# A hybrid decoder step on one core: the first stage's instructions in a fixed order, planned from estimated times, and the cached rows copied in other stages

## The chip, the cores and the metric

The kernel runs on 1 core of one Trainium2 chip. The metric is the device time of one execution in microseconds (us). The engines are PE (TensorE, with its weight loads as PEld), DVE (VectorE), ACT (ScalarE), POOL (GpSimd) and SP, whose queue issues all DMA transfers here. Each engine works through its own instructions in their order; semaphores make it wait for others.

## The reference, cut to what matters

Two layers over 512 prompt tokens and 8 sample tokens, each with its own cached state. Layer 0 mixes by gated DeltaNet, layer 1 by dilated sliding-window attention; each is followed by an MLP with a squared ReLU.

```python
for i in range(DEPTH):                      # DEPTH = 2
    hp, hs = rmsnorm(yp, norm_mix[i]), rmsnorm(ys, norm_mix[i])
    if i % N_MIXERS == 0:
        op, cbp, sp = gdn_mixer(hp, conv0, s0, *wts)
        osm, cbs, ss = gdn_mixer(hs, state_conv[j], state_gdn[j], *wts)
    else:
        op, bufs_p = dsw_prompt(hp, *wts)
        osm, bufs_s = dsw_sample(hs, (cache_kv_w128[j], cache_kv_w512[j], cache_kv_w2048[j]), *wts)
    yp, ys = yp + op, ys + osm
    yp = yp + sqrelu_mlp(rmsnorm(yp, norm_mlp[i]), mlp_w_up[i], mlp_w_down[i])
    ys = ys + sqrelu_mlp(rmsnorm(ys, norm_mlp[i]), mlp_w_up[i], mlp_w_down[i])
```

In `gdn_mixer`, projections give q, k, v, a gate z and two figures per head; q, k and v go through a convolution of width 4 and SiLU. There are 8 q/k heads and 16 value heads. In chunks, the state of each value head follows from an inverse of a unit triangular matrix:

```python
t_inv = triangular_solve(eye + a_strict, eye, lower=True, unit_diagonal=True)
u = t_inv @ (v * beta); w = t_inv @ (kb * exp(gc)); attn = (q @ k.T) * decay
def step(s, inp):                           # one chunk after the other
    v_new = u_c - w_c @ s
    o = qg_c @ s + a_c @ v_new
    s = s * gl_c + kd_c.T @ v_new
```

The sample's k/v buffers are results too: the cached rows, moved up by one where the window is full, and the new row behind them.

## The kernel before, in words

All of it is fp32. A dense projection is made of three matmuls of rounded halves: the weights are split into `whi` (rounded, by ACT) and `wlo` (the rest, by DVE), the tokens likewise, and `proj` (L157) adds high by high, high by low and low by high. A tile of 128 output features and 8 blocks of input is 2 halves of 260 tokens, 24 matmuls each, 48 together. A raw weight tile has 512 KB; three are held (`WB`), and two of each half.

The stages follow each other: `load_x`, `gdn` (layer 0's mixer, the "first stage"), `mlp`, `dsw` (layer 1's mixer, "attention"), `mlp`, `store_x`.

The first stage goes by pairs p = 0 to 7: one q/k head and its two value heads. For each pair:

- `key` (K), `query` (Q) and `values` (V, two tiles) project and convolve by `project` (L505); `gates` (Z, two tiles) makes silu(z).
- `decay` (L588) loads rows of cumulated log-decay from DRAM (`ET<-Dg`), subtracts on DVE (L596), and makes E from the products `kk` of keys with keys.
- `invert` (L622) sends E's diagonal blocks through DRAM (`D<-E`, then `Ft<-D`), solves them on POOL in 62 steps (L638, L641: `fs` and `held`), and sends the result back (`D<-held`, `held<-D`) into the tile `Uf`. `merge` (L649) makes blocks of 64 and 128 on PE (`px`, `pu`).
- `scan` (L698) is the recurrence: per chunk of 128 tokens `pk` on PE, `R` on DVE, `pv` on PE, `vn` on ACT, `pS` and `po` on PE, `S` on DVE.
- `sample` (L796) is the step of the 8 sample tokens: products `sks` with the cached states `S`, then `u` sent through DRAM to all partitions (`sut`, `ut`, `Du`, `ub`) and the states updated on ACT and POOL.
- `out` (L847) is norm, gate and split; `out_proj` (L878) adds the output projection of a pair to the residual stream.

Before pair 0 the stage makes its constants: the small projection `bafm`, its transpose `bat`, beta and the log-decay (with a polynomial on POOL, L451 and L452), the cumulated sums `gc`, their transposes to DRAM (`gcT`, `Dg`) and the sample's figures `sbc`.

What order the instructions take is decided by a scheduler that builds each engine's list from a simulated time line, with raised priority for `decay`, `invert`, `merge`, `scan`, `sample` and `out` (`urgent`, L33). Beside each weight load, `weights` (L134) issues one copy of cached rows from DRAM to DRAM (`kept_rows`, L88; 136 copies of up to 832 KB) once `owed` has gone from -16 to 1. So 52 copies fall in the first stage, 64 in the first MLP and 20 in attention.

In attention, head h's projections stand beside head h-1's scores and values (rounds 0 to 8); the output projections of pairs of heads are made in round 8 (`DOUT`), the last behind it.

Of the kernel before, what the change touches and what calls it, by code (L numbers as in the profile page):

```python
# [10 lines left out]
F32 = mybir.dt.float32  # L11
# [18 lines left out]
HP = {"decay": 2000, "invert": 2000, "merge": 2000, "scan": 2000, "sample": 2000, "out": 2000}  # L30


def urgent(f):  # L33
    def g(self, *a):
        with self.tc.high_priority(HP[f.__name__]):
            return f(self, *a)

    return g

KEEP = 104  # L40
WARM = 24
RAW = 6
SMALL = 1300
WB = (3, 2, 2)
MM = 2
OHB = 8
DOUT = {8: ((0,), (1, 2))}
PACE = dict(gdn=1, mlp0=1, dsw=1, mlp1=1)


class Common:
    """What every stage uses: constants, the residual stream, the weight stream, projections."""

    def __init__(self, ctx, tc, I, O):
# [7 lines left out]
        # what lives as long as the kernel: the residual stream and constants, and the split operand  # L62
# [9 lines left out]
        self.kept, self.owed, self.stage = self.kept_rows(), -16, "gdn"  # L72
        self.gain = {}
# [14 lines left out]
    def kept_rows(self):  # L88
        """The cached rows that stay in the sample's k/v buffers, a piece of them at each step."""
# [18 lines left out]
    def bank(self, name, tag="misc", n=512):  # L108
        return self.ps.tile([P, n], F32, tag=tag, name=name, bufs=self.tags[tag])
# [24 lines left out]
    def weights(self, cols, nk=KT):  # L134
        """cols: DRAM [nk * 128, n] pieces; gives each 128 columns in parts for the products."""
# [3 lines left out]
        for c in cols:  # L139
            for j in range(0, c.shape[1], step):  # L140
# [6 lines left out]
                self.owed += PACE[self.stage]  # L147
                while self.owed >= 1:
                    self.owed -= 1
                    next(self.kept, None)  # L150
# [5 lines left out]

    def proj(self, w, mov, evac, m=P, halves=(0, 1)):  # L157
        nc = self.nc
        nk = len(mov)
        for hf in halves:  # L160
            ps = self.pm.tile([P, H], F32, tag="mm", name="mm", bufs=MM)
            s = slice(hf * H, hf * H + H)
            for k in range(nk):
# [4 lines left out]
            evac(ps[:m], hf, s)  # L168
# [4 lines left out]
    def split_x(self, gain, k, hf, x=None):  # L173
        """The moving operand of the next projection, x * gain, as a rule not normalized yet."""
        nc = self.nc
        x = self.x if x is None else x
        s = slice(hf * H, hf * H + H)
        nc.scalar.activation(self.xh[:, k, s], x[:, k, s], AF.Copy, scale=gain[:, k : k + 1])  # L178
        nc.vector.scalar_tensor_tensor(  # L179
            self.xl[:, k, s], x[:, k, s], gain[:, k : k + 1], self.xh[:, k, s].bitcast(F32), ALU.mult, ALU.subtract  # L180
# [15 lines left out]
    def mean_sq(self, acc):  # L196
        """1 / (mean square + eps) by token: [128, 5], the last column for the sample tokens."""
# [13 lines left out]
    def rsqrt(self, pool, x, eng, tag):  # L211
        """1 / sqrt(x) for positive x [128, n], by Newton's iteration from an estimate made of its bits."""
# [12 lines left out]
    def bcast(self, pool, r, tag="bc"):  # L225
        """A figure by token, [128, 5], over all partitions: [128, T]."""
# [21 lines left out]
    # the tensor engine's clock goes up with use: let it run while the rows come in  # L248
# [107 lines left out]
def gdn(K, l, rms, gain, done):  # L356
# [9 lines left out]
    with ExitStack() as ctx:  # L366
# [4 lines left out]
        for k in range(KT):  # L371
            nc.gpsimd.tensor_tensor(xn[:, k], K.x[:, k], rb, ALU.mult)
# [1023 lines left out]
```

## Time and profile before

| | |
|---|---|
| median of 3 runs | 2167.4 us (2167.13 to 2167.78) |
| span of the profiled execution, its own time | 2168.5 us, 1.1 us over that median |
| PE busy | 1989.6 us (92%) |
| DVE busy | 1349.5 us (62%) |
| ACT busy | 899.4 us (41%) |
| POOL busy | 535.6 us (25%) |
| moved by DMA | 328.54 MB |

All comes from one profiled execution. "Busy" counts time in which an instruction of the engine runs; matmuls overlap each other, so PE's work is better read from the distance of their starts. A line number is that of the kernel, and many lines are those of a helper; names such as `mm<-split,whi` are result and operands. "Waits" name the event that came last before an instruction could start.

### The profile page before, as it was taken

How to read it: one execution, taken by the hardware profiler on the slowest of the kernel's cores; microseconds unless marked ns; L12 is line 12 of the kernel's file. 1: busy time of each engine (PE TensorE's matmuls, PEld its weight loads, DVE VectorE, ACT ScalarE, POOL GpSimd, SP SyncE). 2: the span in 40 equal slices, each digit the busy share in tenths (PEclk: the TensorE clock that was granted, in tenths of full speed). 3: DMA queues.
4: the chain of work that ended last, by engine and by line, in shares of the span. 5: the costliest groups of instructions: out<-in, count | busy, mean ns of one | idle time of the engine just before them, and what ended most of it. 6: DMA issues, size and time to landing. Idle time of an engine off the chain costs nothing. (4 is left out here: it accounts for less than half of the span.)

```text
span 2168.5 us, 41683 instructions
## 1 busy us (share of the span) xinstructions
PE 1989.6 (92%) x16361; PEld 1950.9 (90%) x16361; DVE 1349.5 (62%) x3332; ACT 899.4 (41%) x2416; POOL 535.6 (25%) x821
## 2 busy tenths in 40 slices
PE   7677889896969789999999999999999989999999
PEld 6677778896969679999999999999999989999998
DVE  6754856785766584544556467676766785544544
ACT  5434444444334353223244555555555444233231
POOL 4253264355253230000002133232332250000000
PEclk8889989988979889999999999999999999999999
DMA  5334554764655538666676675534445343333332
GB/s 145 68 71 114 149 157 127 223 181 128 204 150 158 168 96 303 228 238 242 232 248 227 221 242 141 140 108 123 120 128 137 97 115 88 89 98 89 94 92 79
DMA packets 416277, 328.54 MB, mean 152 GB/s; under 512 B 48408, under 2 KB 404568, under 8 KB 413896
## 3 DMA queue, kind: packets, MB, share of 16 engines
q1 hardware_dynamic: 416080, 325.88, 50.4%
q8 instruction: 128, 2.10, 0.4%
q14 instruction: 69, 0.57, 0.1%
HBM read 302.19 MB, written 132.83 MB: 201 GB/s over the span
## 5 line engine op out<-in xcount | busy, mean ns | idle before, releaser
L165 PE MATMUL mm<-split,whi 128*128 128x260 f32 (+1 forms) x2960 | 866.7, 293 | 3.8 <-ACT split L178 2.5
L167 PE MATMUL mm<-split,wlo 128*128 128x260 f32 (+1 forms) x2960 | 851.8, 288 | 9.4 <-DVE wlo L132 9.4
L166 PE MATMUL mm<-split,whi 128*128 128x260 f32 (+1 forms) x2960 | 851.8, 288 | 8.7 <-DVE split L179 8.6
L166 PEld LDWEIGHTS mm<-split,whi 128*128 128x128 f32 (+1 forms) x2960 | 567.1, 192 | 12.3 <-DVE split L179 10.5
L167 PEld LDWEIGHTS mm<-split,wlo 128*128 128x128 f32 (+1 forms) x2960 | 566.5, 191 | 11.8 <-DVE wlo L132 10.9
L165 PEld LDWEIGHTS mm<-split,whi 128*128 128x128 f32 (+1 forms) x2960 | 567.6, 192 | 7.2 <-ACT split L178 3.7
L132 DVE TENSOR_TENSOR wlo<-raw,whi 128x1024 fp32r<-128x1024 f32 (+1 forms) x273 | 341.0, 1249 | 195.3 <-ACT whi L131 177.7
L131 ACT CAST whi<-raw 128x1024 fp32r<-128x1024 f32 (+1 forms) x273 | 285.8, 1047 | 411.7 <-PE mm L166 396.1
L167 PE MATMUL mm<-hh,wlo 128*128 128x260 f32 x1024 | 288.8, 282 | 0.0
L166 PE MATMUL mm<-hl,whi 128*128 128x260 f32 x1024 | 288.8, 282 | 0.0
L165 PE MATMUL mm<-hh,whi 128*128 128x260 f32 x1024 | 288.1, 283 | 0.0
L167 PEld LDWEIGHTS mm<-hh,wlo 128*128 128x128 f32 x1024 | 193.0, 188 | 0.0
L166 PEld LDWEIGHTS mm<-hl,whi 128*128 128x128 f32 x1024 | 192.8, 188 | 0.0
L165 PEld LDWEIGHTS mm<-hh,whi 128*128 128x128 f32 x1024 | 192.3, 188 | 0.0
L335 DVE TENSOR_TENSOR t<-mm,bc 128x260 f32<-128x260 f32 x128 | 54.8, 428 | 153.0 <-PE mm L167 153.0
L191 POOL TENSOR_TENSOR acc<-acc,sq 128x260 f32<-128x260 f32 x42 | 37.8, 909 | 382.0 <-ACT sq L190 381.3
L638 POOL TENSOR_TENSOR fs<-Ft,held 128x60 f32<-128x60 f32 (+24 forms) x248 | 100.5, 405 | 89.2 <-DMA Ft<-D 58.7
L131 ACT CAST hh<-q 128x260 fp32r<-128x260 f32 x128 | 52.5, 410 | 122.1 <-DVE q L322 122.1
L165 PE MATMUL mm<-onh,whi 128*128 128x260 f32 x256 | 90.3, 356 | 13.0 <-DVE base L892 7.9
L530 DVE SCALAR_TENSOR_TENSOR conv<-pre,held,conv 128x512 f32<-128x512 f32 x96 | 77.6, 808 | 30.1 <-POOL pre L508 27.2
L641 POOL TENSOR_TENSOR held<-held,fs 128x60 f32<-128x60 f32 (+24 forms) x248 | 90.5, 365 | 18.5
L132 DVE TENSOR_TENSOR hl<-q,hh 128x260 fp32r<-128x260 f32 x128 | 54.9, 429 | 57.0 <-ACT hh L131 57.0
(374 smaller groups left out, 3319.4 us busy)
## 6 DMA issues: line engine op xcount, KB each, us to landing
out_dram<-in_cache_kv_w_dram SPq DMA_DIRECT2D x112, 832.0 KB
raw<-in_dsw_w_in_dram SPq DMA_DIRECT2D x72, 512.0 KB
raw<-in_mlp_w_up_dram SPq DMA_DIRECT2D x64, 512.0 KB
raw<-in_mlp_w_down_dram SPq DMA_DIRECT2D x64, 512.0 KB
raw<-in_gdn_w_in_dram SPq DMA_DIRECT2D x48, 512.0 KB
S<-in_state_gdn_dram SPq DMA_DIRECT2D x16, 512.0 KB
raw<-in_gdn_w_out_dram SPq DMA_DIRECT2D x16, 512.0 KB
ub<-Du SPq DMA_DIRECT2D x16, 512.0 KB
```

What stands on the lines that cost most here:

```text
L131: nc.scalar.copy(hi, src)
L132: nc.vector.tensor_tensor(lo, src, hi.bitcast(F32), ALU.subtract)
L165: nc.tensor.matmul(ps[:m], lhsT=w[0][:, k, :m], rhs=xh[:, s], start=k == 0, stop=False)
L166: nc.tensor.matmul(ps[:m], lhsT=w[0][:, k, :m], rhs=xl[:, s], start=False, stop=False)
L167: nc.tensor.matmul(ps[:m], lhsT=w[1][:, k, :m], rhs=xh[:, s], start=False, stop=k == nk - 1)
L191: nc.gpsimd.tensor_tensor(acc[:, s], acc[:, s], t, ALU.add)
L335: nc.vector.tensor_tensor(t, ps, r2[:, s], ALU.mult)
L530: nc.vector.scalar_tensor_tensor(a, pre[:, j : j + NP], convw[:, ft, j : j + 1], a, ALU.mult, ALU.add)
L638: nc.gpsimd.tensor_tensor(tmp[:, :m, :n], Ft[:, None, j + 1 :, j].to_broadcast([P, m, n]), Uo[:, :m, j : j + 1].to_broadcast([P, m, n]), A ...
L641: nc.gpsimd.tensor_tensor(Uo[:, :m, j + 1 :], Uo[:, :m, j + 1 :], tmp[:, :m, :n], ALU.add)
```

## The change

In the first stage the scheduler has no say any more. A class `Weave` wraps the engines: each call adds an estimated time to that engine's clock (per-engine constants: a DVE instruction 0.16 us and 0.00106 per element, a POOL one 0.24 and 0.002, a DMA issue 0.1), and instructions stand in the order in which they are called. The dense work is a stream written by hand (`ORDER`). After each k-block of three matmuls the planner looks at the chains (generators that stop at each `yield`) and lets those go on whose inputs are due by its clocks. Loads of raw tiles are issued three ahead, by `fetch`, as the planner reaches them. `LOAD`, `TO_INV` and `FROM_INV` are its figures for a load (6 us), the way of E to POOL (12) and back (9).

Within the stage: the output projections of pairs 0 and 1, 2 and 3, 4 and 5 are made together; key rows are kept as they are (`kt`) and the scan scales `vd` on ACT in place of two `kd` products on DVE; `pS` is one product of 256 columns; small POOL copies (`tail`) and memsets are gone; three PSUM banks rather than two take the projections; osb shares E's tile. Elsewhere: `PACE` sets the copies per weight load (first stage 0, first MLP 1, attention 0.5, second MLP 0.6: 64, 40 and 32 copies), and attention makes the output projection of the first pair of heads in round 6 rather than 8.

Names in the rows: `bat`, `gc`, `gcT`, `sbc` are the constants, `mm` a dense projection, `E`, `D`, `Ft`, `held` the inversion's tiles (`held` also other constants), `S` the sample's states, `raw` a weight tile.

First place: PE, at the constants of the first stage. Before, around `gc`:

```order
L167 MATMUL mm<-split,wlo 128x260
L165 MATMUL mm<-split,whi 128x260
L166 MATMUL mm<-split,whi 128x260
L167 MATMUL mm<-split,wlo 128x260
L463 MATMUL gc<-base,held 128x64
L464 MATMUL gc<-base 128x64
L165 MATMUL mm<-split,whi 128x260
```

Now:

```order
L534 MATMUL bat<-base,bafm 128x32 x4
L534 MATMUL bat<-base,bafm 8x32
L572 MATMUL gc<-base,held 128x64
L573 MATMUL gc<-base 128x64
L579 MATMUL gcT<-base,held 64x128
L598 MATMUL sbc<-sbd,base 128x256
L145 MATMUL mm<-split,wlo 128x260
L145 MATMUL mm<-split,whi 128x260 x2
```

Before, 123 rows of mostly dense products stand between `bat` and `gc`; now none, and the dense stream of K0 (but for its first two products) stands behind `sbc`.

Second place: DVE, at the first subtraction on `ET`. Before:

```order
L783 COPY base<-sst 128x16
L785 COPY base<-sst 128x8
L132 TENSOR_TENSOR wlo<-raw,whi 128x1024
L222 SCALAR_TENSOR_TENSOR base<-base 128x4
L596 TENSOR_TENSOR ET<-ET,held 128x1024
L534 SCALAR_TENSOR_TENSOR conv<-tanh,conv 128x512
```

Now:

```order
L583 TENSOR_TENSOR held<-held 128x64
L599 COPY held<-sbc 128x256
L145 TENSOR_TENSOR ET<-ET,held 128x1024
L145 TENSOR_TENSOR wlo<-raw,whi 128x1024 x2
L145 TENSOR_TENSOR held<-held,bc 128x512
```

Before, K0 is split, projected and convolved when `ET` comes; now the subtraction stands ahead of the split of K0's weights.

Third place: SP, around the inversion's result of a pair. Before (pair 0):

```order
L629 DMA D_576<-E 32x8x32 x4
L632 DMA Ft<-D_576 128x1x1024
L146 DMA raw<-in_gdn_w_in_dram 128x8x128 x3
L642 DMA D_577<-held 4x256x32
L146 DMA raw<-in_gdn_w_in_dram 128x8x128
L646 DMA held<-D_577 32x8x32 x4
```

Now (pairs 0 and 1):

```order
L145 DMA D_1254<-E 32x8x32 x4
L145 DMA Ft<-D_1254 128x1x1024
L145 DMA D_835<-held 4x256x32
L145 DMA held<-D_835 32x8x32 x4
L145 DMA Du<-ut 16x128
L145 DMA raw<-in_gdn_w_in_dram 128x8x128
L145 DMA ub<-Du 128x1024
L145 DMA raw<-in_gdn_w_in_dram 128x8x128 x2
L145 DMA out_dram<-S_1143 128x8x128
```

Raw tiles stand behind stores that wait for POOL (`D_835<-held`, `out_dram<-S_1143`) and behind loads that wait for such stores; the copies of cached rows, which stood among them, are gone from the stage.

The diff's core:

```diff
-HP = {"decay": 2000, "invert": 2000, "merge": 2000, "scan": 2000, "sample": 2000, "out": 2000}
+HOP, LOAD, TO_INV, FROM_INV, BACKLOG = 0.15, 6.0, 12.0, 9.0, 4.0
-MM = 2
-OHB = 8
-DOUT = {8: ((0,), (1, 2))}
-PACE = dict(gdn=1, mlp0=1, dsw=1, mlp1=1)
+MM = dict(gdn=3, mlp0=2, dsw=2, mlp1=2)
+OHB = 6
+DOUT = {6: ((0,),), 8: ((1, 2),)}
+PACE = dict(gdn=0, mlp0=1, dsw=0.5, mlp1=0.6)
+class Weave:
+    def spend(self, eng, us):
+        t = max(self.clk[eng], self.cur + (HOP if self.last not in (eng, None) else 0.0)) + us
+        self.clk[eng], self.cur, self.last = t, t, eng
+    def due(self, c):
+        if not self.done.issuperset(c[4].get("names", ())):
+            return None
+        tag = c[4].get("tag")
+        busy = 0.0 if c[1] < 0 else max(self.clk["vector"], self.clk["scalar"]) - BACKLOG
+        return max(c[0], self.free[tag][self.turn[tag]] if tag else 0.0, busy)
+    def dense(self, steps):
+        self.cur, self.last = self.now, "tensor"
+        for _ in steps:
+            self.pump()
+            self.cur, self.last = self.now, "tensor"
+    def need(self, *names):
+        while not self.done.issuperset(names):
+            t, _, i = min((max(t, self.now), c[1], i) for i, c in enumerate(self.chains) for t in (self.due(c),) if t is not None)
+            self.clk["tensor"] = t
+            self.step(self.chains[i])
+class Timed:
...
+                us = {"vector": 0.16 + 0.00106 * n, "scalar": 0.17 + 0.00087 * n, "gpsimd": 0.24 + 0.002 * n, "sync": 0.1}[self.name]
-        self.kept, self.owed, self.stage = self.kept_rows(), -16, "gdn"
+        self.kept, self.owed, self.stage = self.kept_rows(), 0, "gdn"
-OUTP = {p: [((p - 2,), 0, 8)] for p in range(2, 8)}
-OUTP[8] = [((6,), 0, 8), ((7,), 0, 8)]
-EARLY = (7,)
+ORDER = "K0 Q0 K1 Q1 V0 K2 Q2 Z0 V1 Z1 K3 Q3 V2 K4 Q4 Z2 O01 V3 K5 Q5 Z3 V4 K6 Q6 Z4 O23 V5 K7 Q7 Z5 V6 V7 Z6 O45 Z7 O6 O7"
+        def fetch():
+            if len(raws) < len(tiles):
+                c, nk = tiles[len(raws)]
...
+                nc.sync.dma_start(t, c.rearrange("(k p) n -> p k n", p=P))
+                raws.append((t, W.cur + LOAD))
+                K.keep()
-                kd = self.kd = K.tile(gp, [P, C4, 2, P], F32, tag="kd", name="kd", bufs=2)
-                for v in range(2):
-                    nc.vector.tensor_tensor(kd[:, :, v], pst, egc[:, 2, :, 2 * p + v, None].to_broadcast([P, C4, P]), ALU.mult)
+                kt = self.kt = K.tile(gp, [P, C4, P], F32, tag="kt", name="kt", bufs=2)
+                nc.scalar.copy(kt, pst)
+                    vd = K.tile(gp, [P, 2, P], F32, tag="vd", name="vd", bufs=1)
+                    for v in range(2):
+                        nc.scalar.activation(vd[:, v], pv[:, v * P : (v + 1) * P], AF.Copy, scale=egc[:, 2, c, 2 * p + v : 2 * p + v + 1])
-                    for v in range(2):
-                        nc.tensor.matmul(pS[:, v * P : (v + 1) * P], lhsT=self.kd[:, c, v], rhs=vn[:, v], start=True, stop=True)
+                    nc.tensor.matmul(pS, lhsT=self.kt[:, c], rhs=vd.rearrange("p v d -> p (v d)"), start=True, stop=True)
+        with tc.manual_schedule():
...
+            for name, p in stream:
+                A = pairs[p[0]]
+                W.need(*waits(name, p))
+                W.dense(out_proj(p) if name == "O" else {"K": A.key, "Q": A.query, "V": A.values, "Z": A.gates}[name]())
+            W.need(*[c[3] for c in W.chains])
```

More of the change, by code (lines that the diff above doesn't have):

```diff
@@ L146, in weights @@
                 nc.sync.dma_start(raw, c[:, j : j + m].rearrange("(k p) n -> p k n", p=P))
[L147 to L150, printed above, removed]
+                self.keep()
                 self.split_to(hi, lo, raw)
@@ L155, in weights, with keep, proj_steps @@
         return res
+    def keep(self):
+        self.owed += PACE[self.stage]
+        while self.owed >= 1:
+            self.owed -= 1
+            next(self.kept, None)
     def proj(self, w, mov, evac, m=P, halves=(0, 1)):
+        for _ in self.proj_steps(w, mov, evac, m, halves):
+            pass
+    def proj_steps(self, w, mov, evac, m=P, halves=(0, 1)):
         nc = self.nc
@@ new lines, in prepare @@
+        def prepare(i):
+            raw, at = raws[i]
+            yield when(at=at)
+            nk = tiles[i][1]
+            hi, lo = (K.tile(K.wp, [P, KT * P], F32R, tag=t, name=t, bufs=n).rearrange("p (k n) -> p k n", k=nk) for t, n in (("whi", WB[1]), ("wlo", WB[2])))
+            nc.scalar.copy(hi, raw)
+            yield
+            nc.vector.tensor_tensor(lo, raw, hi.bitcast(F32), ALU.subtract)
+            fetch()
+            ws.append([(hi[:, :, j : j + P], lo[:, :, j : j + P]) for j in range(0, KT * P // nk, P)])
@@ new lines, in get, with project @@
+        def get():
+            i = count[0]
+            W.need(f"w{i}")
+            count[0] += 1
+            if i + 1 < len(tiles):
+                W.launch(prepare(i + 1), f"w{i + 1}", -1)
+            return ws[i]
+        def project(ft, out, then, name, rank):
+            (w,) = get()
+            n = len(raw)
+            if n >= NPRE:
+                W.need(f"pre{n - NPRE}")
+            pre, tn = pres[:, n % NPRE], news[:, ft]
+            def ev(ps, hf, s):
+                nc.scalar.copy(pre[:, 3 + hf * H : 3 + hf * H + H], ps)
+                if hf:
+                    nc.scalar.copy(tn, ps[:, H - NS - 3 :])
+            first = n < RAW
+            raw.append(ft)
+            if len(raw) == RAW:
+                halves = []
+                for hf, s in enumerate((slice(0, H), slice(H, T))):
+                    for k, _ in enumerate(K.proj_steps(w, mov, ev, halves=(hf,))):
+                        if hf:
+                            K.split_x(gain, k, 0, xns[k])
+                        yield
+                for k in range(KT):
+                    K.split_x(gain, k, 1, xns[k])
+                xctx.close()
+            else:
+                yield from K.proj_steps(w, mov, ev)
+            W.launch(conv(n, pre, tn, ft, first, out, then), name, rank)
@@ L882, in out_proj @@
+        def out_proj(ps):
+            step = KT // (2 * len(ps))
             end = ps[-1] == last
             ws = []
-            for c in range(k0, k1, step):
-                ws += zip(range(c, c + step), K.weights([wout[ps[0] * 2 * P : (ps[-1] + 1) * 2 * P, c * P : (c + step) * P]], nk))
-                if not end or c + step == k1:
+            for c in range(0, KT, step):
+                ws += zip(range(c, c + step), get())
+                if not end or c + step == KT:
                     for halves in ((0,), (1,)) if end else ((0, 1),):
+                        if halves == (1,):
+                            W.need(f"out{last}")
```

574 lines of the change are left out of this document (342 added, 232 removed).

## The prediction

> **What bounds the kernel now.** I read the page first. It shows whether one engine is full all the time, and where it is not.
>
> ```profile
> span 2168.5 us, 41683 instructions
> PE   7677889896969789999999999999999989999999
> DVE  6754856785766584544556467676766785544544
> PEclk8889989988979889999999999999999999999999
> ```
>
> From the 16th of 40 slices on (54 us each) PE has nines but for one 8, and its clock is at 9: there PE is the bound. In the first 15 slices nothing is. Second, where the first stage ends (the evacuation of its output projection: durations, first and last start), and the busy times by stage (columns: stretch, then busy time and count of PE, weight loads, DVE, ACT, POOL, then granted clock, DMA share, GB/s).
>
> ```profile
> L892 DVE TENSOR_TENSOR base<-base,mm x125: 409/420/428, 250.4 to 800.4; 128x260 f32<-128x260 f32 x125
> ```
>
> ```profile
> 0.00:60.00 60.00, 44.76 (x313) 40.27 (x314) 38.47 (x95) 27.76 (x70) 27.56 (x47) 0.89 0.52 136
> 60.00:802.00 742.00, 606.36 (x4922) 582.61 (x4923) 503.55 (x1443) 307.74 (x901) 298.82 (x612) 0.86 0.52 145
> 802.00:1170.00 368.00, 368.00 (x3075) 367.57 (x3074) 194.68 (x344) 126.85 (x231) 14.81 (x17) 1.00 0.70 239
> 1170.00:1795.00 625.00, 602.28 (x4983) 592.98 (x4981) 429.78 (x1126) 324.41 (x1024) 194.42 (x146) 1.00 0.51 145
> 1795.00:2168.50 373.50, 368.20 (x3076) 367.52 (x3075) 183.03 (x325) 112.68 (x195) 0.00 (x0) 1.00 0.31 91
> ```
>
> The last evacuation starts at 800.4, so I cut the stages at 802. The MLPs (third and fifth row) run 3075 matmuls in 368 us, 0.12 us each, at full clock. The first stage idles 802 - 651 = 151 us of PE, and its clock is 0.86: only there is time to be had. Third, who keeps PE waiting in 0 to 802 us (columns: total, times, longest):
>
> ```profile
> PE sut L826 <- DVE base L819: 34.5, 5, 13.2
> PE px L660 <- DMA held<-D: 21.4, 3, 11.3
> PE pv L715 <- DVE R L712: 13.7, 4, 8.9
> ```
>
> These are not shortages of work: PE's queue stands behind one small product (the sample's `sut`, the inversion's `px`, the scan's `pv`) with dense matmuls ready behind it. An order with such products later would fill the holes.
>
> **The change part by part.** *PE's work in the first stage* stays, and I need its size. Spacing of starts at full clock:
>
> ```profile
> 695.04 0.61 PE L720 MATMUL pS<-vn,kd 128*128 128x128 f32 x4
> 695.49 0.61 PE L731 MATMUL po<-vn,ET 128*128 128x128 f32 x4
> 695.94 0.60 PE L735 MATMUL po<-S,kq 128*128 128x256 f32 x2
> 696.37 1.84 PE L816 MATMUL sks<-base,S 128*128 128x2 f32 x16
> 698.08 0.37 PE L165 MATMUL mm<-onh,whi 128*128 128x260 f32 x1
> 722.76 0.69 PE L660 MATMUL px<-held,E 32*32 32x32 f32 x16
> 723.38 0.39 PE L165 MATMUL mm<-onh,whi 128*128 128x260 f32 x1
> 1723.95 0.60 PE L1103 MATMUL kf<-base,kt 128*128 128x128 f32 x4
> 1724.39 0.27 PE L1220 MATMUL qbt<-base,smp 128*128 128x128 f32 x1
> ```
>
> Two fp32 products of 128 columns take 0.45 us (four records), one of 256 columns 0.43, sixteen `sks` 1.71, sixteen `px` 0.62, four transposes 0.44. A pair has 32 of the first (7.2 us), 6 of the second (2.6), 16 `sks` (1.7), 24 transposes (2.6), 40 small blocks (1.6) and 16 of 64 by 64, taken as transposes (1.8): 17.5 us, eight pairs 140. Dense: 48 + 16 tiles of 48, 3072 x 0.12 = 368. Together 508 us, in which 734 us pass today (about 68 to 802).
>
> *The start gets worse.* Today K0's dense stream fills PE while the decay's constants are made:
>
> ```profile
> 40.98 0.29 DVE L426 TENSOR_TENSOR held<-bat,base 128x128 f32<-128x128 f32 x1 [0.29 <-PE bat L425]
> 48.17 0.88 POOL L452 TENSOR_SCALAR t<-t 128x80 f32<-128x80 f32 x1
> 56.83 0.35 POOL L451 TENSOR_TENSOR t<-t,t 128x80 f32<-128x80 f32 x1
> 57.27 0.41 POOL L452 TENSOR_SCALAR t<-t 128x80 f32<-128x80 f32 x1
> 59.91 0.41 PE L463 MATMUL gc<-base,held 128*128 128x64 f32 x2 [2.73 <-DVE base L461]
> 69.12 0.93 SPq L595 DMA_DIRECT2D ET<-Dg  x2
> 77.11 1.22 DVE L596 TENSOR_TENSOR ET<-ET,held 128x1024 f32<-128x1024 f32 x1 [4.00 <-DMA ET<-Dg]
> ```
>
> In the new order all but two of K0's matmuls stand behind `gc`, `gcT` and `sbc`, and on DVE K0's `wlo` stands behind the subtraction on `ET`, which waits for its load. `bat` at 41 us; to `gc` 18.9 us today, of which I take off 6: the seven pairs of POOL steps should all go at 0.93 us, as the last one did (56.83 to 57.68 plus a gap), 6.5 in place of 10 (an early step took 0.88, the last 0.41), and DVE has no foreign work between. So `gc` at 53.5, `gcT` and the store to `Dg` by 55.5, the load issued at 57.4, landed 8 us later (69.12 to 77.11) at 65.4, subtraction 1.2 and `wlo` 1.2: the stream starts at **S = 68 us** (64 if the load takes 5, 74 if the constants stay slow).
>
> *First inversion.* Its chain today, pair 0: E stored, inverted on POOL, back, first `px`:
>
> ```profile
> 86.49 1.82 SPq L629 DMA_DIRECT2D D<-E  x4
> 89.72 0.62 SPq L632 DMA_DIRECT2D Ft<-D  x1
> 100.90 0.61 POOL L638 TENSOR_TENSOR fs<-Ft,held 128x31 f32<-128x31 f32 x1 [8.35 <-DMA Ft<-D]
> 130.97 0.59 SPq L642 DMA_DIRECT2D D<-held  x1
> 138.13 0.39 PE L660 MATMUL px<-held,E 32*32 32x32 f32 x4 [11.30 <-DMA held<-D]
> ```
>
> 51.6 us. The planner's own figures for it are 12 + 22 (62 steps of 0.24 plus 0.002 per element) + 9 = 43, so `px` is placed too early, and a strict PE waits there. K0's matmuls take 5.8 us. Up to E the new order gives DVE five steps of 1024 elements (1.2 us, the row on `ET`), twelve of 512 (0.68, the row on `kd` below) and some 29 small ones (0.25, between 0.23 and 0.29): 6 + 8 + 7 = 21, and 2 for changes of engine. So E stands at S + 29, `px` at S + 80.6 = 149. 406 dense matmuls and 8 us of small ones stand ahead: PE is there at S + 57. It waits 24 us, once; later pairs have 50 to 62 us of PE work between their `kk` and `px`, against 52 to 56 us of chain, so 0 to 5 us each. Work left after it: 508 - 57 = 451. **PE's floor for the stage's end: 149 + 451 = 600 us**, 605 with a short tail.
>
> *DVE.* It loses the two `kd` products of a pair (a copy on ACT replaces them) and 48 of 128 evacuations of the output projection (pairs 01, 23 and 45 share one):
>
> ```profile
> L555 DVE TENSOR_TENSOR kd<-kqt,held x16: 674/680/693, 65.2 to 659.1; 128x512 f32<-128x512 f32 x16
> 400.00:500.00 100.00, 93.25 (x749) 90.17 (x749) 78.98 (x227) 43.68 (x135) 44.47 (x89) 0.90 0.70 197
> ```
>
> 48 x 0.42 = 20 and 16 x 0.68 = 11 us. Of 542 us in 0 to 802, 511 are left, 38 of them ahead of S: 473 us after it. For PE's floor DVE would have to be 473 / 537 = 88% busy. Its fullest 100 us today are at 79%, its mean 68%. It is strictly ordered, has no slack in the plan (which prices a 512-element step at 0.70 us), and each lag holds a `pv`, `vtr` or `otr` on PE. I take 80%: 473 / 0.80 = 591, so the **stage ends at 68 + 591 = 659 us, 143 us sooner**. Bounds: 605 (88%) and 764 (68%). ACT (28 + 308 = 336 us before, some 30 more) and POOL (327 us, with fewer steps) stay below.
>
> *Copies of the cached rows.* 64 loads with one copy each cost the DMA engines 0.70 - 0.31 of 370 us (third and fifth row): 2.3 us a copy, and PE stayed at 100%. Attention gets 40 rather than 20, the last MLP 32: shares of about 0.58 and 0.5. Cost 0, cover: the two raw tiles loaded ahead; bounds -1 and +4 us. In the first stage 52 copies go, and with them some of the 8 us of `ET` and `Ft` loads; inside the 80%.
>
> *Attention's end.* One output projection (96 matmuls, 11.5 us) moves from the last head to the sixth round. The last round's chain, from the sample's first transposes to its last product:
>
> ```profile
> 1771.30 0.39 PE L1274 MATMUL sav<-held,A 128*128 128x8 f32 x2
> 1775.46 0.51 PE L165 MATMUL mm<-oh,whi 128*128 128x260 f32 x2 [0.68 <-ACT oh L131]
> ```
>
> From 1724.4 to 1771.3 it lasts 47 us and PE idled only some 6 of them. Without 11.5 us of cover it idles 11.5 more; in the sixth round at most 3 us of holes take it up. Cost **+9 us** (bounds 0, if the chain shortens with DVE's lighter load, and +12).
>
> Sum, on the profiled execution's 2168.5 us: -143 + 9 = 2034.5; the median of the runs is 1.1 us lower, so 2033.
>
> [...] At 60 to 802 us the granted clock was 0.86. [...] POOL's `L452` step took 0.88 us once and 0.41 another time, in the rows above. [...]
>
> **The rivals.** *PE's floor* (chance 0.14): the order is good enough for DVE at 88%. For it: single 20 us stretches of DVE are full today. Against: no 100 us are. Time: 2168.5 - 197 + 9 - 1 = 1979.
>
> *Order without gain in filling* (0.12): DVE's waits come from its chains, not from the scheduler, and its share stays 68%. For it: the estimates are too low for POOL (22 against 30 us) and `ET` (6 against 8). Against: the copies and many POOL steps between are gone. End at 764: 2168.5 - 38 + 9 - 1 = 2138.
>
> *The weights' queue stops, slower than before* (0.06). SP issues every load in order, and today it waits for POOL:
>
> ```profile
> SPq L642 <- POOL held L641: 37.6, 4, 15.0
> SPq L839 <- POOL S L838: 25.7, 5, 9.3
> ```
>
> In the new order raw tiles stand behind the inversion's store and the states' stores, which the plan prices at 0.1 us. Three raw tiles cover 3 x 5.8 = 17 us. If SP stands from `Ft`'s issue to the store (41 us in the rows above: 130.97 - 89.7) PE starves 24 us a pair, and DVE with it, since its splits need the same tiles: seven pairs, +168: 2201. It decides from 17 + 134 / 7 = 36 us of block on. Against: longest today 15.0.
>
> That the change does nothing (0.02) is hardly possible: every queue of the stage is reordered.
>
> **How the numbers follow.** Forecast 0.66 at 2033, its own range 1990 to 2085 (DVE 86% to 73%). The range 1970 to 2105 takes in PE's floor, 0.14, and leaves the two slow cases out, 0.18. Within 0.2% (4.3 us, about what a measurement of this kernel can tell from no change): 0.02. Faster: 0.66 + 0.14 + 0.12 = 0.92; slower 0.06.
>
> **What would show it.** Right: PE idle from about 41 to 68 us, then one wait of some 24 us on `px`; the first `hh` of the MLP about 140 us sooner; DVE at about 80% from 70 to 650 us; later stages as now, with 5 to 12 us more idle at attention's end. Wrong: waits of `px` over 10 us in later pairs, waits of SP over 17 us followed by `whi` waiting for `raw`, a granted clock below 0.86, or a stage that ends before 620 or after 700 us.

## The result, and the profile after

| | before | after |
|---|---|---|
| median of 4 runs | 2167.6 us (2167.1 to 2168.6) | 2192.0 us (2190.9 to 2194.3) |
| span of the profiled execution | 2168.5 us | 2189.1 us |
| PE, from the span's start to the MLP's first `hh`: busy / idle | 698.8 / 150.9 us | 698.7 / 144.0 us |
| first `hh` of the first MLP | 849.7 us | 842.7 us |
| attention, from the last `hh` to its last `ss` | 624.3 us | 650.8 us |

The ratio is 1.0112 (95% interval 1.0098 to 1.0126): 24 us slower, where 134 us faster was forecast, and outside the range. The first stage gained 7 us in place of 143, attention lost 26.5 in place of 9, and the two MLPs together 1: -7 + 26.5 + 1 is the 20.6 us between the spans, within 0.1.

First the page of the changed kernel, its 40 slices (54.7 us each).

```profile
span 2189.1 us, 41614 instructions
PE   5768998898988789999999999999999969999999
DVE  4675866768576665454554666767675765544444
PEclk7879879999889789999999999999999989999999
```

From the 3rd to the 15th slice PE and its clock look much as before. New are the 5 at the front and one 6 at attention's end, the 33rd slice. Second, the busy times by stage, in the columns of the prediction's table.

```profile
0.00:65.00 65.00, 27.93 (x165) 22.47 (x165) 28.19 (x67) 23.31 (x59) 22.95 (x41) 0.69 0.33 86
65.00:797.00 732.00, 626.37 (x5038) 601.69 (x5039) 507.17 (x1416) 333.86 (x987) 288.90 (x555) 0.87 0.39 102
803.00:1172.00 369.00, 368.47 (x3074) 368.12 (x3072) 192.29 (x339) 128.16 (x227) 14.02 (x24) 1.00 0.66 222
1172.00:1815.00 643.00, 601.63 (x4912) 592.29 (x4911) 421.42 (x1121) 322.04 (x1018) 191.23 (x134) 0.97 0.56 166
1815.00:2189.10 374.10, 368.79 (x3077) 368.11 (x3076) 182.69 (x324) 112.14 (x194) 0.00 (x0) 1.00 0.49 158
```

From the stream's start at 65 us on, the first stage takes 732 us; PE is busy for 626 of them at a clock of 0.87, DVE for 507, 69%. Copies have moved from the first stage (DMA share 0.52 before, 0.39 now) to attention and the last MLP, which takes 374.1 us where it took 373.5.

Third, what PE waits for from there on (columns as in the prediction: total, times, longest).

```profile
PE mm L145 <- DVE wlo L145: 30.6, 13, 11.4
PE otr L145 <- DVE E L145: 22.9, 5, 6.7
PE vtr L145 <- DVE vf L145: 17.5, 4, 11.6
PE pu L145 <- ACT held L145: 10.2, 2, 5.5
PE one L145 <- DVE S L145: 7.1, 2, 6.4
```

The waits shown before (`sut` 34.5 us, `px` 21.4) are gone, as the order promised. In their place stand `wlo`, `otr`, `vtr` and `pu`, nearly all late on DVE; 11.4 us of `wlo`'s are the start itself. PE's idle time from the start (68 us before, 65.3 now) to the first `hh` fell from 135 to 107 us, and ahead of it rose from 16 to 37: of the 28 us won in order, 21 were paid at the start.

Fourth, PE at that start, and the first inversion's end.

```profile
50.86 0.66 PE L572 MATMUL gc<-base,held 128*128 128x64 f32 x2 [12.47 <-DVE base L570]
65.27 0.59 PE L145 MATMUL mm<-split,wlo 128*128 128x260 f32 x1 [11.37 <-DVE wlo L145]
130.52 1.12 PE L145 MATMUL vtr<-base,vf 128*128 128x128 f32 x4 [11.62 <-DVE vf L145]
153.11 0.66 PE L145 MATMUL px<-held,E 32*32 32x32 f32 x16 [1.41 <-DMA held<-D]
```

`gc` came at 50.9 (forecast 53.5), the stream at 65.3 (68), the first `px` at 153.1 (149). Fifth, PE in attention's last round, where 14.7 us pass in one wait.

```profile
1765.73 0.22 PE L1496 MATMUL mxb<-base,mr 1*128 1x1 f32 x1 [0.60 <-DVE mr L1495]
1780.67 0.59 PE L1512 MATMUL sav<-held,A 128*128 128x8 f32 x2 [14.72 <-DVE A L1510]
```

### The profile page after: what moved, and what is told of

Read it like the earlier page. It is cut to its first block, busy times and chain, and to the rows that moved or that the text cites. A ratio compares the mean times of both kernels' runs of the same rounds, so it can differ in the third digit from the quotient of the medians.

```text
span 2189.1 us, 41614 instructions
## 1 busy us (share of the span) xinstructions
PE 1998.4 (91%) x16297; PEld 1957.4 (89%) x16297; DVE 1335.8 (61%) x3271; ACT 922.7 (42%) x2488; POOL 519.6 (24%) x757
## 4 chain that ended last, share of the span: by engine, by line
PE 58%; DVE 12%; DMA 4%; ACT 3%; issue 3%; POOL 2%; SPq 0%; DVEq 0%; ACTq 0%; POOLq 0%
PE mm L277 15%; PE mm L275 15%; PE mm L276 15%; PE mm L145 5%; DVE base L145 2%; DMA X<-base 1%; DVE wlo L233 1%; PE po L1441 1%; DVE wlo L145 1%; PE one L145 1%; PE tr L1294 1%; DVE base L1368 1%; PE sks L145 1%; DVE base L1481 1%; ACT P L1369 1%
## 5 line engine op out<-in xcount | busy, mean ns | idle before, releaser
L275 PE MATMUL mm<-split,whi 128*128 128x260 f32 (+1 forms) x2192 | 635.6, 290 | 3.2 <-ACT split L292 2.0
L276 PE MATMUL mm<-split,whi 128*128 128x260 f32 (+1 forms) x2192 | 624.7, 285 | 7.4 <-DVE split L293 7.4
L277 PE MATMUL mm<-split,wlo 128*128 128x260 f32 (+1 forms) x2192 | 625.4, 285 | 4.8 <-DVE wlo L233 4.8
L276 PEld LDWEIGHTS mm<-split,whi 128*128 128x128 f32 (+1 forms) x2192 | 415.0, 189 | 9.5 <-DVE split L293 9.1
L275 PEld LDWEIGHTS mm<-split,whi 128*128 128x128 f32 (+1 forms) x2192 | 415.1, 189 | 5.3 <-ACT split L292 2.7
L277 PEld LDWEIGHTS mm<-split,wlo 128*128 128x128 f32 (+1 forms) x2192 | 414.2, 189 | 6.2 <-DVE wlo L233 5.8
L232 ACT CAST whi<-raw 128x1024 fp32r<-128x1024 f32 (+1 forms) x209 | 217.8, 1045 | 407.6 <-PE mm L276 397.8
L233 DVE TENSOR_TENSOR wlo<-raw,whi 128x1024 fp32r<-128x1024 f32 (+1 forms) x209 | 256.1, 1225 | 171.9 <-ACT whi L232 163.9
L145 PE MATMUL mm<-split,whi 128*128 128x260 f32 x1536 | 321.7, 309 | 1.1 <-ACT split L145 0.8
L145 PEld LDWEIGHTS mm<-split,whi 128*128 128x128 f32 x1536 | 259.6, 204 | 4.7 <-ACT split L145 1.0
L145 PE MATMUL mm<-split,wlo 128*128 128x260 f32 x768 | 229.8, 299 | 28.7 <-DVE wlo L145 28.7
L145 PEld LDWEIGHTS mm<-split,wlo 128*128 128x128 f32 x768 | 156.8, 204 | 31.4 <-DVE wlo L145 31.4
```

What stands on the lines that cost most here:

```text
L145: return real(*a, **k)
L232: nc.scalar.copy(hi, src)
L233: nc.vector.tensor_tensor(lo, src, hi.bitcast(F32), ALU.subtract)
L275: nc.tensor.matmul(ps[:m], lhsT=w[0][:, k, :m], rhs=xh[:, s], start=k == 0, stop=False)
L276: nc.tensor.matmul(ps[:m], lhsT=w[0][:, k, :m], rhs=xl[:, s], start=False, stop=False)
L277: nc.tensor.matmul(ps[:m], lhsT=w[1][:, k, :m], rhs=xh[:, s], start=False, stop=k == nk - 1)
```

## The experiments

Times are medians; ratios are to the kernel before, run beside each group (2169.3 us beside e1 to e4, 2170.0 beside e5 to e8, 2169.2 beside e9 to e12, 2168.3 beside e13 to e16, 2173.1 beside e17 and e18). First `hh` and attention are read from the profile of one execution each. The first `hh` is the first MLP's first product on `hh` in every kernel, so it measures the first stage whatever is done to attention.

| run | median us | ratio to before (95%) | first `hh` | attention |
|---|---|---|---|---|
| the change | 2192.0 | 1.0112 (1.0098 to 1.0126) | 842.7 | 650.8 |
| e1 tail alone, on before | 2189.8 | 1.0086 (1.0062 to 1.0110) | 846.2 | 645.9 |
| e2 copies back | 2192.3 | 1.0097 (1.0069 to 1.0126) | 848.9 | 646.4 |
| e3 scheduler's order | 2209.4 | 1.0181 (1.0157 to 1.0206) | 862.1 | 653.7 |
| e4 constants in the stream | 2183.2 | 1.0065 (1.0042 to 1.0089) | 823.0 | 646.7 |
| e5 idle filled | 2224.1 | 1.0246 (1.0217 to 1.0275) | 869.2 | 657.1 |
| e6 a third of dense out | 2166.5 | 0.9988 (0.9970 to 1.0005) | 811.3 | 656.7 |
| e7 two conv steps out | 2176.1 | 1.0025 (1.0005 to 1.0046) | 821.4 | 646.5 |
| e8 PE priced higher | 2245.4 | 1.0328 (1.0291 to 1.0365) | 881.4 | 670.4 |
| e9 half inversions | 2181.1 | 1.0055 (1.0038 to 1.0071) | 835.3 | 655.5 |
| e10 third `ET` | 2219.6 | 1.0239 (1.0216 to 1.0263) | 862.4 | 667.3 |
| e11 its control | 2206.8 | 1.0176 (1.0160 to 1.0193) | 842.5 | 665.1 |
| e12 third `ET`, on before | 2170.1 | 1.0006 (0.9988 to 1.0023) | 846.9 | 632.8 |
| e13 e6 and e9 together | 2148.8 | 0.9909 (0.9887 to 0.9932) | 792.3 | 657.0 |
| e14 latencies as measured | 2224.6 | 1.0267 (1.0246 to 1.0288) | 873.9 | 651.0 |
| e15 tail back | 2175.0 | 1.0035 (1.0021 to 1.0049) | 845.8 | 635.4 |
| e16 e4 with tail back | 2167.8 | 1.0008 (0.9987 to 1.0029) | 845.9 | 635.6 |
| e17 e6, planned anew | 2214.6 | 1.0190 (1.0148 to 1.0231) | 852.3 | 668.4 |
| e18 latencies near zero | 2288.2 | 1.0519 (1.0477 to 1.0560) | 923.3 | 669.9 |

Some of these scatter more than the change (2190.9 to 2194.3): e4 lay between 2168.1 and 2194.7, e6 between 2159.2 and 2174.1, e7 between 2165.3 and 2184.9, e16 between 2161.9 and 2181.7. A profile shows one execution; for e4 and e7 it is the fastest of ten, for e16 the second slowest. So single figures from profiles need a margin. The first stage of e1 is that of the kernel before (846.2 and 849.7), that of e15 the change's (845.8 and 842.7): 3 to 4 us apart. That of e16 is e4's, and lies 23 us from it (845.9 and 823.0). e12 has attention's PE products in the order of the kernel before, and takes 632.8 for 624.3.

**The tail (e1, e15) and the copies (e2).**

```diff
 e1, on before; the reverse on after is e15 (there with 2 buffers for kc and vc)
-OHB = 8
-DOUT = {8: ((0,), (1, 2))}
+OHB = 6
+DOUT = {6: ((0,),), 8: ((1, 2),)}
```

> The kernel before, with only attention's output projections moved as in the change: pair 0 in round 6 (and 6 buffers in place of 8). In the changed kernel attention is 26.5 us longer, from the last hh of the first MLP to the last ss. Theory, cover: the last head's chain lost 11.5 us of dense work, so PE stands before the sample's sav (14.7 us in the changed kernel's trace), before po (about 3) and runs the rest at a lower clock (about 3): 2167.5 + 15 to + 22, with a wait of 10 to 15 us before sav. Rival, copies: the 52 copies that left the first stage slow attention's own loads, the move costs little: 2167.5 + 0 to + 5. What was on record as a cost of this edit is + 9.

> The changed kernel with attention's output projections as before (pair 0 in round 8, 8 buffers), and, so that they have room, 2 buffers in place of 3 for the sample's cached keys and values. Theory, cover: the loss of the tail goes, 2192 - 16 to - 24, and sav's wait of 14.7 us with it. Rival: part of attention's loss is of another kind (copies, two buffers fewer now): 2192 - 0 to - 10.

Measured: e1 is 20.5 us slower, with the same wait. This is PE in e1, the kernel before but for that one edit:

```profile
1776.40 0.60 PE L1274 MATMUL sav<-held,A 128*128 128x8 f32 x2 [14.15 <-DVE A L1272]
```

and PE in e15, the changed kernel with the edit taken back:

```profile
1779.67 0.29 PE L1512 MATMUL sav<-held,A 128*128 128x8 f32 x2
```

There `sav` waits for nothing, and the time is 17 us lower than the change's. Cover is shown as the cause of the larger part of the loss (`OHB` went with `DOUT` both times). Of the 11 us by which e15's attention still exceeds the kernel before, 3 are idle time of PE and 8 slower matmuls: PE is busy 610 us for 602, at a clock of 0.98 for 1.00. e12's attention, 8.5 us longer, shows the same at 0.99. So neither the copies nor the missing third buffer is shown as the cause.

```diff
-PACE = dict(gdn=0, mlp0=1, dsw=0.5, mlp1=0.6)
+PACE = dict(gdn=1, mlp0=1, dsw=1, mlp1=1)
-        self.kept, self.owed, self.stage = self.kept_rows(), 0, "gdn"
+        self.kept, self.owed, self.stage = self.kept_rows(), -16, "gdn"
```

> The changed kernel with the copies of cached rows where they were before (52 in the first stage, 64 in the first MLP, 20 in attention). Theory, cover: attention's loss stays but for 0 to 6 us, and the first stage gets 0 to 8 us slower by slower loads of ET, S and Ft: 2192 - 6 to + 8. Rival, copies: attention gets most of its 26.5 us back: 2192 - 15 to - 22.

Measured: 2192.3, no change. In its profile attention is 4.4 us shorter and the first stage 6.2 longer, no more than profiles scatter. Moving the copies cost the total nothing, as was predicted.

**The order and the start (e3, e4, e16).**

```diff
 e3
-        with tc.manual_schedule():
+        with ExitStack():
 e4: from the polynomial's first step to sbc, in steps of a generator
+        def consts():
+            ...
+            yield when(tag="misc")
+            ps = K.bank("gc")
+            ...
-                yield when(p > 1 and f"scan{p - 2}")
+                yield when("consts", p > 1 and f"scan{p - 2}")
+            W.launch(consts(), "consts", -1)
```

> The changed kernel's instructions of the first stage, but their order left to the scheduler (no fixed order; no raised priorities). Theory: the planned order is worth something by itself: from the stream's start on, PE's idle time fell from 134 to 100 us, so the scheduler's order gives this back, 2192 + 20 to + 45. Rival: the fixed order is what holds the stage up (each engine stands behind the planner's wrong estimates), and the scheduler's order of the same steps is faster: 2192 - 10 or less.

> The changed kernel, with the making of the decay constants (from the polynomial to sbc) put into the planned part as a chain of its own, so that the first key and query projections stand before gc, gcT and sbc again. Theory, start: PE's 26 us of extra idle time before 65 us go, and nothing else takes their place: 2192 - 15 to - 25. Rival, first inversion: the chain from the constants to the first px is what the start waits for, PE runs out of dense work before it comes, and the wait only moves to px or vtr: 2192 - 5 to + 3.

> The run with the decay constants put into the planned stream, with attention's output projections as before and 2 buffers for the sample's cached keys and values. Theory: both effects add, 2183.2 - 16 to - 24, that is 2159 to 2167: level with the kernel before or up to 8 us better. Rival: the gain at the start is not robust (its runs lay from 2168 to 2195): 2170 or more.

e3: 17 us slower than the change, a little under what was expected. So the planned order is worth something against the scheduler's on the same instructions, without the raised priorities that the kernel before had; PE's waits behind 65 us in e3 show what it removes:

```profile
PE px L145 <- DMA held<-D: 52.0, 5, 18.9
PE one L145 <- DVE R L145: 19.5, 8, 12.0
PE one L145 <- ACT vn L145: 17.8, 8, 6.9
```

e4: 9 us faster than the change by its median, between the two theories. PE in e4's fastest run:

```profile
50.11 0.66 PE L145 MATMUL gc<-base,held 128*128 128x64 f32 x2 [3.27 <-DVE base L145]
105.51 1.12 PE L145 MATMUL kqt<-base,kq 128*128 128x128 f32 x4 [12.68 <-DVE kq L145]
```

The wait before `gc` is mended, and a new one of the same length stands at 105 us, before the keys' transposes. e16 puts both repairs together: level with the kernel before (1.0008, 0.9987 to 1.0029). Nothing here beats it clearly while doing the whole of the work.

**Which engine holds the first stage (e6, e7, e17).**

```diff
 e6 (in proj_steps, first stage only); e17 without the spend, and DOUT = {4: ((0,),), 6: ((1,),), 8: ((2,),)}
+                if slot:
+                    self.weave.spend("tensor", 0.12)
+                else:
                     nc.tensor.matmul(ps[:m], lhsT=w[1][:, k, :m], rhs=xh[:, s], start=False, stop=k == nk - 1)
 e7 (in conv)
-                nc.vector.scalar_tensor_tensor(a, pre[:, j : j + NP], convw[:, ft, j : j + 1], a, ALU.mult, ALU.add)
+                if j == 2:
+                    nc.vector.scalar_tensor_tensor(a, pre[:, j : j + NP], convw[:, ft, j : j + 1], a, ALU.mult, ALU.add)
+                else:
+                    W.spend("vector", 0.7)
```

> The changed kernel with the high-by-low-weights third of the first stage's dense products left out (1024 matmuls, 123 us at 0.12 us each), the order of all that remains unchanged. Theory: in the first stage PE at its granted clock is the main bound (632 of the 738 us after the stream's start are PE busy), so most goes with them: 2192 - 90 to - 140. Rival: the chains over DVE and ACT in their fixed order set the pace, and PE waits instead: 2192 - 20 to - 60.

> The changed kernel with two of the convolution's three accumulating steps left out (64 DVE steps of 0.82 us, 52 us of 539), the order of all that remains unchanged. Theory: PE is the main bound, DVE is late only here and there: 2192 - 10 to - 30. Rival: DVE in its fixed order sets the pace: 2192 - 40 to - 60.

> The changed kernel without the high-by-low-weights third of the first stage's dense products, and the planner knows it, so that the order is made for it (earlier run: the order as made for the whole). Attention's output projections of pairs 0 and 1 in rounds 4 and 6, for room; so read the first hh. The planner's own end of the stage is 670 with the third left out and 669 with it. Theory, the plan's chains over DVE and ACT set its length and not PE: first hh no sooner than with the old order, 811 - 10 to + 20. Rival, the fixed order is in the way: an order for the lighter PE gives most of the 123 us, first hh at 790 or less.

The theory that PE at its granted clock is the bound falls. In e6 the stage shrinks by 31 us for 123 us of matmuls left out (the median by 25.5). Its stage, in the columns of the table by stage:

```profile
65.00:766.00 701.00, 535.62 (x3958) 503.60 (x3959) 511.41 (x1417) 331.03 (x988) 289.60 (x555) 0.79 0.41 106
```

PE's busy time falls by 91 us, not 123, since its clock falls too, from 0.87 to 0.79, and its waits grow by 60 of these 91. Planned anew for the lighter PE (e17) the stage is no shorter than with all the matmuls, 852.3 against 842.7, and misses both ranges that were expected:

```profile
65.00:809.00 744.00, 543.11 (x3964) 503.88 (x3964) 499.17 (x1420) 335.01 (x991) 293.19 (x556) 0.76 0.41 100
```

Here PE waits 201 us of 744. The planner says as much by its own sum: its stage ends 669 us after its zero with the third and 670 without. DVE alone isn't the bound either: of its 52 us e7 returned 16 by the median, 21 in its fastest run.

**A loop through the inversion (e9 to e13).** The loads of `ET` on SP's queue for pairs 2 to 4 in the changed kernel:

```profile
189.20 0.36 SPq L145 DMA_DIRECT2D ET<-Dg  x1
265.88 0.46 SPq L145 DMA_DIRECT2D ET<-Dg  x1
352.16 0.43 SPq L145 DMA_DIRECT2D ET<-Dg  x1
```

and the last states of pairs 0 to 2 on its DVE:

```profile
187.33 0.60 DVE L145 SCALAR_TENSOR_TENSOR S<-S,held,one 128x128 f32<-128x128 f32 x2 [1.45 <-PE one L145]
264.83 0.59 DVE L145 SCALAR_TENSOR_TENSOR S<-S,held,one 128x128 f32<-128x128 f32 x2
350.67 0.59 DVE L145 SCALAR_TENSOR_TENSOR S<-S,held,one 128x128 f32<-128x128 f32 x2
```

Each load stands about 1 us behind the scan that frees its buffer, in the kernel before as well. I took this for the bound.

```diff
 e9 (in invert); e13 is e6 and e9
                 for j in range(31):
+                    if j % 2:
+                        ...
+                        continue
 e10; e12 is the ET line alone, on before; e10 and e11 also have RAW = 4 and e17's DOUT
-                yield when(p > 1 and f"scan{p - 2}")
-                ET = self.ET = K.tile(gp, [P, U, P], F32, tag="ET", name="ET", bufs=2)
-                kt = self.kt = K.tile(gp, [P, C4, P], F32, tag="kt", name="kt", bufs=2)
+                yield when(p > 2 and f"scan{p - 3}")
+                ET = self.ET = K.tile(gp, [P, U, P], F32, tag="ET", name="ET", bufs=3)
+                kt = self.kt = K.tile(gp, [P, C4, P], F32, tag="kt", name="kt", bufs=3)
```

> The changed kernel with 15 of the 31 pairs of POOL steps of each inversion left out, the order of all that remains unchanged. POOL has 290 us of 738 to do and is no bound by its share. Theory, loop: ET has two buffers, its load for pair p starts when the scan of pair p - 2 ends (in the changed kernel's trace 1 us behind it or less, six times of six), and from that load over E, the inversion and the merge to the scan's end pass 146 to 191 us; four such loops in series make the stage. Some 13 us off each inversion is then 4 x 13 off the stage: first hh at 842.7 - 40 to - 65. Rival, no loop (PE's or DVE's work or the strict order sets the pace): 842.7 - 0 to - 15.

> The changed kernel with a third buffer for ET and for kt, the planner told so (the load of ET behind the scan of pair p - 3), and, to make room for them, the tokens split behind four projections in place of six and attention's output projections of pairs 0 and 1 in rounds 4 and 6. To be compared with the next run, which has the same but two buffers. Theory, loop: with three pairs in the loop the stage is no longer held by it: first hh 20 to 60 us sooner than in the next run. Rival: the strict order of the engines holds it where it is, since the planner, with its short latencies, sees no loop (its own end of the stage is 673 with three buffers, 669 with two): within 12 us of the next run.

> The control of the run before: the changed kernel with the tokens split behind four projections and attention's output projections of pairs 0 and 1 in rounds 4 and 6, two buffers of ET and kt as in the change. Expected by all theories: first hh within 12 us of 842.7, attention (last hh to last ss) 5 to 20 us longer than the changed kernel's 650.8 by the cover theory, unchanged by the rival that copies slow attention.

> The kernel before with a third buffer for ET, nothing else. In its trace too the load of ET for pair p stands behind the scan's end of pair p - 2 (208.4 and 210.1, 276.0 and 275.8, 355.6 and 355.4, 437.5 and 437.3, 522.7 and 528.2, 601.9 and 601.7). Theory, loop: 2167.5 - 15 to - 60. Rival, another two-buffer tile (Uf, vt, E, the states) or its order holds the loop as well: 2167.5 - 8 to + 8.

> The changed kernel with both cuts of earlier runs: the high-by-low-weights third of the first stage's dense products left out, and 15 of the 31 pairs of POOL steps of each inversion; order unchanged. Alone they gave 31 us (first hh 811.3) and 11 us (no more than that) of the changed kernel's 842.7. Theory, two limits side by side: each alone uncovered the other, so together they give clearly more than the sum of 42: first hh 842.7 - 65 to - 95. Rival, each is diluted for itself by the waits of a strict order: the sum, 842.7 - 35 to - 50.

The theory falls three times. e9 returns 11 us of the 40 to 65 (7 in its profile). e10, in which the small figures of a pair still have two places and so can be those of a later pair, reaches the first `hh` 20 us later than its control e11, where 12 either way was the rival's range; e12 changes nothing. A load that starts when a buffer comes free isn't yet what the stage waits for. (e11 confirms the tail once more: another 11.5 us of cover less, attention 14 us longer.) e13 returns 50 us in its profile and 43 by its median: near the sum of its parts (31 and 7 in profiles, 25.5 and 11 by medians), and not the 65 or more of two limits that hide each other.

**The clock, and the planner's prices (e5, e8, e14, e18).**

```diff
 e5: where the planner leaves PE idle for t
+                for _ in range(int(t / 0.22)):
+                    W.real.tensor.matmul(idle[:, :P], lhsT=ident, rhs=ident, start=True, stop=True)
 e8: PE's prices; DOUT as in e17
+                us *= 1.16
 e14; e18, which has e17's DOUT as well
-HOP, LOAD, TO_INV, FROM_INV, BACKLOG = 0.15, 6.0, 12.0, 9.0, 4.0
+HOP, LOAD, TO_INV, FROM_INV, BACKLOG = 0.15, 8.0, 23.0, 13.0, 4.0
+HOP, LOAD, TO_INV, FROM_INV, BACKLOG = 0.05, 3.0, 3.0, 3.0, 4.0
```

> The changed kernel, with dummy products of a constant (128 by 128, some 0.2 us each, 499 of them) on PE wherever the planner itself leaves PE idle; nothing reads them. In the changed kernel the first stage's dense products lose 63 us at about half rate (0.22 us in place of 0.12). Theory, clock after idling: the filled gaps keep the clock up, a third to half of that loss goes: 2192 - 20 to - 40. Rival: the slow stretches stand behind the small products and behind waits that the planner did not foresee, and the dummies only delay: 2192 - 5 to + 20.

> The changed kernel with PE's steps priced 1.16 times as high in the planner (its 549 us of PE work become 637, near the 632 that PE is busy in the trace; its own end of the stage goes from 669 to 728 us after its zero), so that the other engines' steps stand where they would be ready; and attention's output projections of pairs 0 and 1 in rounds 4 and 6. First stage, theory: PE's 100 us of waits after the start come from an order planned for a faster PE and fall by 20 us or more, the first hh at 842.7 - 15 to - 35. Rival: the waits come from the chains' latencies and not from PE's price: the first hh within 10 us of 842.7. Attention, by the cover theory: 11.5 us less cover in the last head, so 10 to 15 us more from the last hh to the last ss than the changed kernel's 650.8.

> The changed kernel, its planner's latencies as measured: 8 us for loads (6), 23 up to POOL's part of the inversion, which takes in that its 62 steps last some 8 us longer than planned (12), 13 behind it (9). Its own end of the stage goes from 669 to 705 us. Theory: the strict order is early with what waits for an inversion, the waits of PE (100 us behind the start) come from that: first hh 842.7 - 15 to - 35. Rival: the latencies are there whatever the planner thinks, the order is merely honest: 842.7 - 10 to + 10.

> The changed kernel with the planner's latencies near zero (0.05 us between engines, 3 us for loads and either side of the inversion; 0.15, 6, 12 and 9 in the change); attention's output projections of pairs 0 and 1 in rounds 4 and 6, for room. The planner's own end of the stage goes from 669 to 654. Theory, the plan's length carries over to the chip: first hh 842.7 - 10 to - 20 (longer latencies made it 31 us later). Rival: what is placed too early makes the strict engines wait: 842.7 + 10 to + 40.

e5, its first stage:

```profile
65.00:824.00 759.00, 705.37 (x5940) 681.49 (x5941) 508.00 (x1418) 334.93 (x988) 285.74 (x556) 0.94 0.38 98
```

The clock rises from 0.87 to 0.94 as PE's waits fall from 106 to 54 us, so here it does hang on PE's gaps; but the dummies add 79 us of PE time, and the stage ends 27 us later. The other three miss in the same way: with PE priced near its measured work the stage is 39 us longer, with measured latencies 31, with latencies near zero 81. The planner's own ends for them are 728, 705 and 654 against 669 with the change's prices, so neither a more honest nor a shorter plan was a shorter stage. All four lie outside every range that was expected of them.

## Why the prediction was wrong, point by point

**"These are not shortages of work ... An order with such products later would fill the holes": this step failed.** The order did move the products that PE stood before, and PE's idle time behind the start fell by 28 us of 135; the rest came back before other products, late on DVE. e6 and e17 show that PE's dense work is not what the stage is short of time for: with a third of it gone the stage is 31 us shorter in the old order, and no shorter in an order made for it. That PE's waits are only the sign of late chains of small steps over DVE, ACT, POOL and DMA is argued from this, not shown. No single cut frees the stage (52 us off DVE gave 16 to 21, some 12 off each inversion 7 to 11, 123 off PE 25 to 31, the start 9). Which dependence sets the sum stays open; nor was another `ORDER`, or another rule by which the planner lets chains go on, tried.

**PE's work of 508 us, and the floor of 600: mis-sized.** The dense products' spacing was taken at full clock. In the changed kernel PE is busy 626 us between 65 and 797, at a clock of 0.87: with no wait its work would end at 65 + 626 = 691. Of these 626 us it ran 143 at half the clock, by the trace's clock records, so about 72 of the 118 us that 508 lacks are the clock, an estimate. What makes up the rest was not taken apart; busy time also counts a product to its own end, where the prediction counted to the next start (0.61 us and 0.45 in its row on `pS`).

**DVE at 80%: failed.** Behind the start it is busy 507 of 732 us, 69%, as before (68%). The work taken off was counted rightly in instructions: the evacuations of the output projection are 80 of 420 ns before the first `hh`,

```profile
L145 DVE TENSOR_TENSOR base<-base,mm 128x260 f32<-128x260 f32 x80 | 32.7, 419 | 10.4 <-PE mm L145 9.7
```

48 fewer than 128. The durations of all DVE steps in the first 802 us fell from 632 to 595 us when added up, yet the time in which DVE has at least one in hand fell only from 542 to 539, since fewer overlap. DVE got no fuller, and POOL's steps `fs` got no longer; they took 0.39 us on average, 0.41 before (the first row is the kernel before's):

```profile
L638 POOL TENSOR_TENSOR fs<-Ft,held 128x60 f32<-128x60 f32 (+24 forms) x248 | 100.5, 405 | 89.2 <-DMA Ft<-D 58.7
L145 POOL TENSOR_TENSOR fs<-Ft,held 128x60 f32<-128x60 f32 (+24 forms) x248 | 97.7, 394 | 71.8 <-DMA Ft<-D 53.1
```

**What the plan itself says was left out.** The planner counts 549 us of PE work and 111 us of idle behind the first product, and ends 669 us after its zero, which lies at 56 us of the trace (its first step on `ET`, 6.7, is the one at 62.9). That is 725; the forecast of 659 lay below the plan that it spoke of. The other 72 us of the miss (to 797, the last dense product of the stage) are the chip falling behind the plan: trace time less planned time is 56 us at DVE's first step, 57 at step 240 of 1416 (planned for 133 us), 82 at step 600 (292), 102 at step 1020 (469) and 129 at step 1320 (623). The first 130 us hold; from then on the stage runs 15% slower than planned, without a jump.

**The start:** right in place and size (S at 65.3 for 68). The wait of 24 us at the first `px` came as 11.6 at `vtr` and 1.4 at `px`. The mark of the stage's end was misread: the list that gave 800.4 ended at 802, and the last evacuation before starts at 804.9 (800.6 now).

**Copies:** right, cost 0 within the scatter (e2).

**Attention's end, +9 (0 to 12): the mechanism right, the size not.** e1 measures 20.5. PE's idle time in attention rose by 18.7 us (22.7 to 41.4): 14.7 before `sav`, 3 before `po`, and small waits elsewhere. The sample's chain, from its first transposes at 1736.4, lasts 44 us (47 before), and all its cover was used up at 1766. What was missed beside it is slower matmuls: PE's busy time in attention rose by 8 us, from 601.6 to 609.4. The last 75 us of attention run at a clock of 0.84, where it was 1.00, most of that in the wait itself and for 5.5 us behind it (first all 75 us, then the wait, then what follows it):

```profile
1740.00:1815.00 75.00, 52.40 (x384) 49.26 (x383) 50.53 (x128) 31.06 (x76) 35.07 (x28) 0.84 0.39 109
1766.00:1781.00 15.00, 0.33 (x2) 0.33 (x2) 8.46 (x16) 0.62 (x3) 9.36 (x8) 0.50 0.22 58
1781.00:1786.50 5.50, 4.57 (x20) 3.76 (x19) 0.72 (x4) 0.79 (x2) 0.00 (x0) 0.51 0.00 0
```

Over the first stage the clock and PE's idle time go together, by the tables of stretches: behind the start PE idles 54 us at a clock of 0.94 in e5, 106 at 0.87 in the changed kernel, 136 at 0.86 in the kernel before, 165 at 0.79 in e6 and 201 at 0.76 in e17. Though the longest waits before went, its idle time fell by 30 us only, and the clock hardly moved. Which waits cost clock, and how much, was not measured.

**The rivals.** "Order without gain in filling" named what happened in the first stage, DVE's share staying at 68%, with 0.12; that its chains kept it there is not shown; its price (stage end 764) was 33 us short. "The weights' queue stops" had the sign and not the mechanism: SP stands often, but because raw tiles are full,

```profile
SPq L145 <- DVE wlo L145: 314.7, 45, 22.4
SPq L145 <- DMA D<-held: 57.6, 8, 11.6
```

and in the lists of waits between 65 and 797 us no split (`whi`, `wlo`) waits for a raw tile.

## What to carry to other kernels

An engine's waits name where its queue stands, not what is short: before a gain is booked from filling them, ask how much shorter the stage would be if that engine had a third less to do: here 31 us of 123, and nothing once the order was made anew. Where an order comes from a planner, add up its own end first; a forecast below the plan needs a reason, and the chip fell 15% behind this one. And dense work moved away from a long chain of small steps was paid for more than in full: 20.5 us for 11.5, in idle time and in slower matmuls.

## What the runs showed of the hardware that was not expected

PE's granted clock fell when PE had less to do: 0.87 with all the first stage's matmuls, 0.79 and 0.76 with a third left out, 0.94 with the gaps filled by dummies. So of the 123 us that e6's matmuls take at 0.12 us each, 32 went into slower ones among the rest, an estimate. And one order can scatter over 27 us from run to run (e4). The kernel before lay within 1.5 us beside the change and over 20.6 beside e17 and e18, so that the change's 3.4 us says little of its order; what makes the difference was not tried.
